# First down product kept ungated until the second's evacuation, with the modulation dots and two norms rescheduled

## The chip, the cores and the metric

The kernel runs as one program on one core of one Trainium2 chip. The metric is the device time of one execution in microseconds. The chip's engines are TensorE (PE in the profile, its weight loads PEld), VectorE (DVE), ScalarE (ACT), GpSimd (POOL) and SyncE (SP, which here only issues DMAs; "SPq" in the trace is its queue of issues).

## The reference, cut to what matters

One layer of a diffusion backbone works on 512 latent tokens `x` and 256 context tokens `ctx`, 1024 channels each. A modulation vector of nine sections of 1024 numbers is computed from a conditioning vector for x, and from another for ctx; the change touches how and when those sections are computed, and the first feed-forward sublayer with its residual and norm:

```python
mod_x = (jax.nn.silu(c) @ w_ada + b_ada).reshape(bsz, N_MOD, 1, d)
mod_c = (jax.nn.silu(c_ctx) @ w_ada + b_ada).reshape(N_MOD, 1, d)

def ffn_sublayer(h, m, i, w_up, w_down):
    shift, scale, gate = sub_mod(m, i)            # sections 3i, 3i+1, 3i+2
    y = swiglu(modulate(h, shift, scale), w_up, w_down)
    return post_ln(DEEPNORM_ALPHA * h + 0.5 * gate * y, ln_g[i], ln_b[i])

x = ffn_sublayer(x, mod_x, 0, ffn1_w_in, ffn1_w_out)
ctx = ffn_sublayer(ctx, mod_c, 0, ffn1_w_in, ffn1_w_out)
... = split_proj(modulate(x, shift_x, scale_x) @ w_in)   # z, q, k, v, gates, from sections 3 and 4
```

After that come neighbourhood attention and a gated delta rule, their merge, and a second feed-forward sublayer on x. The hidden width of the feed-forward is 2816, which is 22 tiles of 128. Everything is float32.

## The kernel before, in words

**Products.** A float32 product is made of three reduced products: an operand is split into a high part (a cast on ACT, L137: `wh`, `uh`, `hx`) and a low part (a subtraction on DVE, L139: `wl`, `ul`), and PE runs high by high, high by low and low by high. Each 128x1024 weight tile (512 KB) is loaded on SP (L174, helper `Stream`) into a raw tile `wr`, a ring of two slots in the pool `wp`, then cast and subtracted.

**Modulation.** A modulation section of 1024 is eight columns of 128, and each column is one step: a 512 KB piece of `w_adaT` is loaded (L296, on SP) and multiplied and summed along the row with the conditioning row on DVE (L280, 128x1024; one such "dot" for x and, for sections 2 to 4, a second for ctx). The generator `ada_gen` gives 48 such steps, for sections 2 to 7 in order; section 2 is the gate of this sublayer, 3 and 4 modulate the projections, and 5 to 7 are used later. Calls of `ada_step(n)` place them by hand: one or two per pass of the first loop, two in the context loop, two behind the last weights of the first down product, then by the tables ADA2 and ADA3. A finished gate section is turned into a row and stored by `rows_out` (`to_row`, L239).

**Stages around the change**, in order:

1. The x loop (L456): hidden tiles 3 to 7 of x, 512 tokens wide (tiles 0 to 2 are done earlier), with the context's own modulation `modulate_k` in between, and one ada step a pass (two in the last).
2. The context loop (L476): hidden tiles 0 to 7 for 256 tokens, with an ada step after tiles 0 and 2, then the row of gate section 2.
3. The first down product (L574): these 8 hidden tiles times their down weights, first x in 8 PSUM banks (4 token tiles by 2 halves), then ctx in 4. `down` (L196) keeps the banks open over all weights; its last KL weights, the tail, are taken token tile by token tile so that the banks end one after another. The evacuation loads the token rows (L584) and the gate row (`load_g`), and DVE forms alpha times token plus gate times product (L588, L589), which goes to the DRAM tile `accd`.
4. "Seven" (L606): the other 14 hidden tiles by a seven-product scheme; an ada step is placed by ADA2 after each. Hidden activations go to DRAM.
5. The second down product, x (L703): 14 hidden tiles come back (`hx`, loaded on SP by `h_next`), eight weights with all 8 banks, then a tail of six. Behind each of the eight weights `h_next` issues loads of later `hx` and `hc` tiles, of `accd` (tile `ax`, L697) and the ada steps of ADA3; their raw tiles are a ring of four of their own.
6. Evacuation `evac1`: per half a multiply by the gate (L635) and an add of `accd` with row sums (L636); then the norm `finish1` (two passes of 128x1024 on DVE, L649 and L651, with squares on ACT, L644, and the inverse root on POOL) and the modulated, transposed activations `u2` (transposes L148 on PE, L151 on ACT, then the split into `uxh` and `uxl`).
7. The second down product for ctx (L726) runs on PE meanwhile; FIN1 says behind which weights the four `finish1` and `u2` of x are issued. Its banks are evacuated in the same way into `x1c`.
8. The projections `z` (L1002), which read `uxh` and `uxl` of all four x tiles, then attention and the rest.

The program's order on each engine is fixed when it is built, by a scheduler that starts from the order of the code; DMA loads on SP are issued in SP's order, each when its slot is free.

## Time and profile before

| what | value |
|---|---|
| runs of the kernel | 1517.03, 1508.75, 1510.5 us; median 1510.5 |
| profiled execution | 1512.61 us, its span 1510.8 us |
| mean granted TensorE clock | 0.986 |
| DVE busy | 1149.5 us, 76% of the span |
| ACT busy | 662.8 us, 44% |
| DMA | 248.56 MB, mean 165 GB/s |

How to read the views in this document: a page's section 1 gives the busy time of each engine; a table by windows gives for each stretch of the span its length, the busy time (and count) of PE, PEld, DVE, ACT and POOL in us, the granted clock of PE, the busy share of the DMA engines and the GB/s that they moved. A chain of waits is followed back from the end of a stretch, a line for each piece: start, length, what ran or was waited for. A row of waits reads "engine, line <- what it waited for: us in total, times, longest". A group of instructions has line, engine, operation, tiles and shapes, count | busy us, mean ns of one | idle time before them and what ended it. A busy PE is not PE at its peak rate, so matmul counts per stretch say more than its busy share.

### The profile page before, as it was taken

The numbers are of one execution on the slowest core, as the hardware profiler recorded it, in microseconds if no ns is written. First come the engines' busy times: TensorE is split into PE (matmuls) and PEld (weight loads), VectorE is DVE, ScalarE is ACT, GpSimd is POOL, SyncE is SP. The second block draws the span as 40 slices with busy tenths as digits, with TensorE's granted clock in tenths as the row PEclk, the third lists the DMA queues.
The fourth block names the chain that finished last, engine by engine and source line by source line (L and its number), as shares of the span: only waits on it lengthen the run. The fifth ranks groups of instructions, "written<-read, shape, count | busy, mean of one in ns | idle before, by whom it ended". The sixth has DMA issues, their size and how long they took to land.

```text
span 1510.8 us, 23895 instructions
## 1 busy us (share of the span) xinstructions
PE 1441.6 (95%) x9117; PEld 1262.9 (84%) x9117; DVE 1149.5 (76%) x1975; ACT 662.8 (44%) x1090; POOL 211.2 (14%) x262
## 2 busy tenths in 40 slices
PE   6998999999999989999996998989999999999997
PEld 4778989999997778889875777867778999998886
DVE  8787869999988665778677795567669699886626
ACT  5433524434333386555534334267526454444310
POOL 1000000000000110313201001333221022220001
PEclk9999999999999999999998999999999999999999
DMA  9677664445469444222576514274344143233732
GB/s 375 207 262 232 209 236 171 156 164 167 165 231 397 157 153 134 92 78 91 175 214 183 168 64 124 72 261 146 100 168 144 60 136 107 98 112 121 269 98 83
DMA packets 114948, 248.56 MB, mean 165 GB/s; under 512 B 35145, under 2 KB 50577, under 8 KB 114833
## 3 DMA queue, kind: packets, MB, share of 16 engines
q1 hardware_dynamic: 110192, 229.40, 45.4%
q0 software_dynamic: 3056, 12.33, 2.2%
q10 hardware_dynamic: 1586, 5.32, 0.9%
q8 instruction: 71, 1.16, 0.3%
q14 instruction: 43, 0.35, 0.1%
HBM read 215.50 MB, written 31.50 MB: 163 GB/s over the span
## 4 chain that ended last, share of the span: by engine, by line
PE 69%; DVE 13%; DMA 10%; issue 4%; ACT 3%; POOL 1%; SPq 1%; DVEq 0%; ACTq 0%; POOLq 0%
PE ps L211 15%; PE ps L533 4%; PE ps L535 4%; PE ps L534 4%; PE pm L192 4%; PE pm L193 4%; PE pm L194 4%; PE ps L193 3%; PE ps L192 3%; PE ps L1679 3%; PE ps L194 3%; PE ps L1680 3%; PE ps L1681 3%; PE pc L1049 2%; DVE wl L139 2%
## 5 line engine op out<-in xcount | busy, mean ns | idle before, releaser
L139 DVE TENSOR_TENSOR wl<-wr,wh 128x1024 fp32r<-128x1024 f32 (+1 forms) x184 | 226.8, 1238 | 119.2 <-ACT wh L137 119.0
L137 ACT CAST wh<-wr 128x1024 fp32r<-128x1024 f32 (+1 forms) x184 | 185.9, 1015 | 265.7 <-PE pm L193 60.1
L192 PE MATMUL pm<-uxh,wh 128*128 128x512 f32 x320 | 132.4, 414 | 1.0 <-ACT spill L798 1.0
L194 PE MATMUL pm<-uxh,wl 128*128 128x512 f32 x320 | 127.2, 397 | 0.3 <-DVE wl L139 0.3
L193 PE MATMUL pm<-uxl,wh 128*128 128x512 f32 x320 | 127.1, 397 | 0.0
L211 PE MATMUL ps<-wh,hx 128*128 128x512 f32 x352 | 96.1, 391 | 0.9 <-ACT wh L137 0.9
L211 PEld LDWEIGHTS ps<-wh,hx 128*128 128x128 f32 x352 | 65.9, 188 | 15.3 <-ACT wh L137 1.3
L280 DVE SCALAR_TENSOR_TENSOR adap<-wr,crow 128x1024 f32<-128x1024 f32 x61 | 74.6, 1223 | 2.3 <-DMA wr<-in_w_adaT_dram 1.7
L192 PE MATMUL ps<-uh,wh 128*128 128x256 f32 (+1 forms) x208 | 68.6, 331 | 5.0 <-ACT wh L137 5.0
L194 PEld LDWEIGHTS pm<-uxh,wl 128*128 128x128 f32 x320 | 61.1, 191 | 14.3 <-DVE wl L139 1.3
L192 PEld LDWEIGHTS pm<-uxh,wh 128*128 128x128 f32 x320 | 61.5, 192 | 12.6 <-ACT spill L798 1.4
L193 PEld LDWEIGHTS pm<-uxl,wh 128*128 128x128 f32 x320 | 61.4, 192 | 10.6
L114 POOL TENSOR_TENSOR rs<-ve,mhalf 128x1 f32<-128x1 f32 (+2 forms) x46 | 48.2, 1050 | 140.7 <-DVE ve L110 138.3
L193 PE MATMUL ps<-ul,wh 128*128 128x256 f32 (+1 forms) x208 | 67.5, 326 | 0.0
L194 PE MATMUL ps<-uh,wl 128*128 128x256 f32 (+1 forms) x208 | 66.6, 325 | 0.0
L193 PE MATMUL ps<-uxl,wh 128*128 128x256 f32 (+1 forms) x192 | 61.6, 324 | 2.1 <-DVE uxl L139 2.1
L192 PE MATMUL ps<-uxh,wh 128*128 128x256 f32 (+1 forms) x192 | 60.7, 323 | 1.6 <-ACT uxh L137 1.4
L194 PE MATMUL ps<-uxh,wl 128*128 128x256 f32 (+1 forms) x192 | 61.1, 321 | 0.0
L137 ACT CAST wh<-ra 128x1024 fp32r<-128x1024 f32 x31 | 32.6, 1053 | 58.1 <-PE ps L534 20.2
L533 PE MATMUL ps<-ur,wh 128*128 128x384 f32 x168 | 56.5, 336 | 0.0
L534 PE MATMUL ps<-ur,wh 128*128 128x384 f32 x168 | 56.4, 336 | 0.0
L533 PE MATMUL ps<-uh,wh 128*128 128x384 f32 x168 | 56.4, 336 | 0.0
(498 smaller groups left out, 4264.4 us busy)
## 6 DMA issues: line engine op xcount, KB each, us to landing
wr<-in_w_adaT_dram SPq DMA_DIRECT2D x64, 512.0 KB, 4.8
wr<-in_up_dram SPq DMA_DIRECT2D x56, 512.0 KB, 3.7
wr<-in_win_dram SPq DMA_DIRECT2D x52, 512.0 KB, 3.4
wr<-in_dn_dram SPq DMA_DIRECT2D x51, 512.0 KB, 4.0
ra<-in_up_dram SPq DMA_DIRECT2D x24, 512.0 KB, 4.2
rb<-in_up_dram SPq DMA_DIRECT2D x18, 512.0 KB, 3.3
ra<-in_w_adaT_dram SPq DMA_DIRECT2D x16, 512.0 KB, 5.0
wr<-in_w_o_dram SPq DMA_DIRECT2D x8, 512.0 KB, 4.5
```

Source lines behind the costliest of these rows:

```text
L114: G.tensor_tensor(rs[:], ve[:], mhalf[:, 0:n], ALU.pow)
L137: S.copy(hi, src)
L139: marks["lo"] = V.tensor_tensor(lo, src, hi.bitcast(F32), ALU.subtract).ins
L192: T.matmul(ps, a, uh[:, k, :], start=(k == 0), stop=False)
L193: T.matmul(ps, a, ul[:, k, :], start=False, stop=False)
L194: marks["mm"] = T.matmul(ps, b, uh[:, k, :], start=False, stop=(k == nk - 1)).ins
L211: T.matmul(banks[t][d][:, c0:c1], a[:, sl], b[:, d * 512 + c0:d * 512 + c1], start=first and j == 0, stop=last and j == 2)
L280: V.scalar_tensor_tensor(pr[:], raw[:], 1.0, crow, op0=ALU.mult, op1=ALU.mult, accum_out=col[:, c:c + 1])
L533: T.matmul(ps[:], a, mh, start=k == 0, stop=False)
L534: T.matmul(ps[:], a, ml, start=False, stop=False)
L535: T.matmul(ps[:], b, mh, start=False, stop=k == 3)
L1679: T.matmul(ps[:], a, uh[:, k], start=k == 0, stop=False)
```

## The change

The first down product is no longer gated where it is made. ACT copies its 12 half tiles out of PSUM (`S.copy`, 128x512), and they go to `accd` as they are; the token and gate loads and the 24 DVE operations of that place go. In `evac1` each half now takes three DVE operations: product plus stored product, times gate, then alpha times token plus that, with row sums (new lines 628, 629, 630). The token rows are loaded there: `xr`, one tile, for x; a slot of the weights' `wr` ring for ctx.

The ada steps move: none in the x loop and the context loop (8 steps, 16 dots of section 2, were there), three in the first down product's tail, one in its context part, 21 instead of 25 in Seven, 16 instead of 13 in the second down product, and five new ones in the z loop. Gate section 2 is finished in Seven, and its rows are stored after Seven's fifth tile. The raw tiles of the ada steps in the second down product are now two tiles of their own and, every third time, a slot of the weights' ring; in the z loop they all use the weights' ring, and the dots read a copy of the conditioning row spread by a DMA (`arow`).

In the second down product, x tiles 0 and 1 are evacuated in the tail's own code, and their norms are issued ahead of the evacuations of tiles 2 and 3. FIN1 becomes (0, 2, 4, 6).

```diff
-    def ada_gen(tps, raw_of, crow):
+    rows_of = [lambda w: crow[:, w]]
+
+    def ada_gen(tps, raw_of):
...
-                        dot_cols(tps[0], raw, crow[:, w], col, sec * 8 + k, sec > 4)
+                        dot_cols(tps[0], raw, rows_of[0](w), col, sec * 8 + k, sec > 4)
...
-    ADA2 = (2, 1, 2, 1, 2, 1, 2, 2, 2, 2, 2, 2, 2, 2)
-    ADA3 = (2, 2, 2, 2, 2, 2, 2, 2)
+    ADA2 = (2, 1, 1, 2, 1, 1, 2, 1, 1, 2, 1, 2, 2, 2)
+    ADA3 = (2,) * 8
...
@@ -458,7 +460,6 @@
             modulate_k(pp, "c", k)
-        ada_step(1 + (f == N1 - 1))
@@ -476,8 +477,6 @@
         ffn_unit(tp, pp, ws.get(), ws.get(), uch, ucl, NCT, *hc[-1])
-        ada_step(f in (0, 2))
-    rows_out(tp, "fs", 2)
@@ -488,8 +487,14 @@
         else:
             ada_step()
-        if j == 0:
-            load_g(0)
+
+    def t_dots(j):
+        if j == 3:
+            ada_step()
+
+    def t_tail(t, j, banks):
+        if j == 1 and t < 3:
+            ada_step()
@@ -563,30 +568,16 @@
-    def load_g(w):
-        g[:] = [tl(tp, [P, 512], "fs", 2) for _ in range(2)]
...
-        if kind == "c":
-            load_g(1)
-        banks, tail = down(pp, ws, hs, n, 2 if kind == "x" else 0, tail if kind == "c" else (), between=t_sums if kind == "x" else None)
+        banks, tail = down(pp, ws, hs, n, 2 if kind == "x" else 0, tail if kind == "c" else (), between=t_sums if kind == "x" else t_dots, after=t_tail if kind == "x" else None)
...
-            nc.sync.dma_start(xr, tok_src(kind, t))
-            tmp = tl(tp, [P, D], "adap")
             for d in range(2):
-                sl = slice(d * 512, (d + 1) * 512)
-                V.tensor_tensor(tmp[:, sl], banks[t][d][:], g[d][:], ALU.mult)
-                V.scalar_tensor_tensor(xr[:, sl], xr[:, sl], ALPHA, tmp[:, sl], op0=ALU.mult, op1=ALU.add)
+                S.copy(xr[:, d * 512:(d + 1) * 512], banks[t][d][:])
             nc.gpsimd.dma_start(accd[t + 4 * (kind == "c")], xr)
@@ -614,6 +605,9 @@
         ada_step(ADA2[f], "h")
+        if f == 4:
+            with tc.issue_after(marks["mm"]):
+                rows_out(sgp, [8, P], "row")
@@ -627,13 +621,13 @@
-    def evac1(p, banks, acc, out, g):
+    def evac1(p, banks, acc, tok, g):
         out_sum, nm = tl(p, [P, 2], "os", 6), tl(p, [P, 1], "nm", 6)
         for d in range(2):
             sl = slice(d * 512, (d + 1) * 512)
-            h = tl(p, [P, 512], "h1", 2)
-            V.tensor_tensor(h[:], banks[d][:], g[:, sl], ALU.mult)
-            V.scalar_tensor_tensor(out[:, sl], h[:], 1.0, acc[:, sl], op0=ALU.mult, op1=ALU.add, accum_out=out_sum[:, d:d + 1])
+            V.tensor_tensor(acc[:, sl], banks[d][:], acc[:, sl], ALU.add)
+            V.tensor_tensor(acc[:, sl], acc[:, sl], g[:, sl], ALU.mult)
+            V.scalar_tensor_tensor(acc[:, sl], tok[:, sl], ALPHA, acc[:, sl], op0=ALU.mult, op1=ALU.add, accum_out=out_sum[:, d:d + 1])
@@ -695,44 +689,75 @@
+        if j == 7:
+            x_row()
         ada_step(ADA3[j])
 
+    xrs = []
+
+    def x_row():
+        xrs.append(tl(lp, [P, D], "xr"))
+        with tc.issue_after(marks["raw"]):
+            nc.sync.dma_start(xrs[-1][:], tok_src("x", len(xrs) - 1))
+
+    raws3 = [0]
+
+    def raw3():
+        raws3[0] += 1
+        k = raws3[0] % 3
+        return tl(ad, [P, D], f"w{k}") if k else tl(wp, [P, D], "wr", WB)
+
-    ada_tp[0], ada_raw[0] = ad, lambda: tl(ad, [P, D], "wr", 4)
+    ada_tp[0], ada_raw[0] = ad, raw3
     h_split(4)
-    bx, tail = down(pp, ws, hx, 4, KL1, between=h_next, n=N2)
+    nms = []
+
+    def x_after(t, j, banks):
+        if j == KL1 - 1 and t < 2:
+            nms.append(evac1(lp, banks, accx[t], xrs[t], gx))
+            x_row()
+
+    bx, tail = down(pp, ws, hx, 4, KL1, between=h_next, after=x_after, n=N2)
     h_split_c(N2)
-    for _ in ada:
-        pass
...
-    nms = [evac1(lp, bx[t], accx[t], accx[t], gx) for t in range(4)]
-    rows_out(lp, "h1", 2)
+    y1s = []
+    for t in range(2):
+        y1s.append(finish1(fc, "x", t, accx[t], nms[t]))
+        with tc.issue_after(marks["x2"]):
+            nms.append(evac1(lp, bx[t + 2], accx[t + 2], xrs[t + 2], gx))
+        if t == 0:
+            x_row()
+    rows_out(wp, [P, D], "wr", WB)
...
     def between(j):
         if j in FIN1:
             t = FIN1.index(j)
-            u2(fc, pp, "x", t, finish1(fc, "x", t, accx[t], nms[t]))
+            u2(fc, pp, "x", t, y1s[t])
+            if t < 2:
+                y1s.append(finish1(fc, "x", t + 2, accx[t + 2], nms[t + 2]))
 
     def after(t, j, banks):
         if j == NT - 1:
-            nms.append(evac1(lp, banks, x1c[t], x1c[t], gc))
+            raw = tl(wp, [P, D], "wr", WB)
+            nc.sync.dma_start(raw[:], tok_src("c", t))
+            nms.append(evac1(lp, banks, x1c[t], raw, gc))
 
-    FIN1 = (0, 2, 5, 8)
+    FIN1 = (0, 2, 4, 6)
...
@@ -837,6 +862,10 @@
+    arow = tl(ga_, [P, D], "arow")
+    nc.gpsimd.dma_start(arow[:], sild.broadcast_to([P, D]))
+    rows_of[0], ada_raw[0] = lambda w: arow[:], lambda: tl(wp, [P, D], "wr", WB)
...
         for _ in fill_spill(ga_, "z", m, zd):
             pass
+        ada_step((2, 2, 1, 0)[m])
```

**SP's order in the second down product, x.** Before, between the sixth weight of the product (`wr_4325`, just above this piece) and the eighth (`wr_4423`); `in_dn` are its weights, `in_w_adaT` the ada steps, `accd` the stored first product, `hd` hidden activations:

```order
L697 DMA ax_719_4075<-accd_1646 128x1024
L680 DMA hc_4461<-hd_2182 128x256
L174 DMA wr_4374<-in_dn_dram 128x1024
L697 DMA ax_720_4076<-accd_1646 128x1024
L680 DMA hx_4404<-hd_2182 128x512
L296 DMA wr_4270<-in_w_adaT_dram 128x1024
L296 DMA wr_4274<-in_w_adaT_dram 128x1024
L296 DMA wr_4319<-in_w_adaT_dram 128x1024
L680 DMA hx_4453<-hd_2182 128x512
L296 DMA wr_4322<-in_w_adaT_dram 128x1024
L680 DMA hx_4500<-hd_2182 128x512
L174 DMA wr_4423<-in_dn_dram 128x1024
```

The same piece now, between the sixth weight (`wr_4268`, just above) and the eighth (`wr_4366`):

```order
L691 DMA ax_701_4018<-accd_1586 128x1024
L298 DMA wr_4311<-in_w_adaT_dram 128x1024
L298 DMA w_754_4262<-in_w_adaT_dram 128x1024
L298 DMA w_755_4265<-in_w_adaT_dram 128x1024
L674 DMA hx_4446<-hd_2114 128x512
L174 DMA wr_4317<-in_dn_dram 128x1024
L691 DMA ax_702_4019<-accd_1586 128x1024
L298 DMA wr_4363<-in_w_adaT_dram 128x1024
L298 DMA w_763_4314<-in_w_adaT_dram 128x1024
L298 DMA w_770_4360<-in_w_adaT_dram 128x1024
L174 DMA wr_4366<-in_dn_dram 128x1024
```

Three ada loads and the last `hx` load moved ahead of the seventh weight, and one of every three ada loads takes a slot (`wr`) of the ring that the weights use. Counted over SP's order from the last of Seven's weight loads on, 13.89 MB are issued up to the seventh weight before and 16.25 MB now; up to the eighth weight 17.83 MB before and 18.87 MB now; up to the ninth 18.87 and 19.92.

**DVE's order at the end of the context part.** Before (`h` and `x1c` are the two evacuations, `uxl_4691<-u_929` the low part of the last x tile's activations, `wl` the low part of a z weight; those of the first two z weights stand two rows above this piece):

```order
L139 TENSOR_TENSOR uxl_4691<-u_905_4970,uxh_4690 128x4x128
L635 TENSOR_TENSOR h_935_5135<-ps_4747,g_4740 128x512
L139 TENSOR_TENSOR uxl_4691<-u_905_4970,uxh_4690 128x4x128
L636 SCALAR_TENSOR_TENSOR x1c_842_4742,os_5130<-h_934_5132,x1c_842_4742 128x512
L636 SCALAR_TENSOR_TENSOR x1c_842_4742,os_5130<-h_935_5135,x1c_842_4742 128x512
L637 TENSOR_SCALAR nm_5131<-os_5130 128x1
L635 TENSOR_TENSOR h_938_5165<-ps_4748,g_4740 128x512
L635 TENSOR_TENSOR h_939_5168<-ps_4749,g_4740 128x512
L636 SCALAR_TENSOR_TENSOR x1c_843_4743,os_5163<-h_938_5165,x1c_843_4743 128x512
L649 SCALAR_TENSOR_TENSOR x1c_842_4742<-x1c_842_4742,nm_5131,lng_4695 128x1024
L636 SCALAR_TENSOR_TENSOR x1c_843_4743,os_5163<-h_939_5168,x1c_843_4743 128x512
L139 TENSOR_TENSOR uxl_4691<-u_929_5071,uxh_4690 128x4x128
```

Now, from the evacuation of the last two banks (`ps_4756`, `ps_4757`) to the first z weight's low part (`wl_5139`):

```order
L628 TENSOR_TENSOR x1c_809_4667<-ps_4756,x1c_809_4667 128x512
L628 TENSOR_TENSOR x1c_809_4667<-ps_4757,x1c_809_4667 128x512
L629 TENSOR_TENSOR x1c_809_4667<-x1c_809_4667,g_4750 128x512 x2
L643 SCALAR_TENSOR_TENSOR x1c_808_4666<-x1c_808_4666,nm_5093,lng_4673 128x1024
L630 SCALAR_TENSOR_TENSOR x1c_809_4667,os_5127<-wr_5125,x1c_809_4667 128x512
L139 TENSOR_TENSOR uxl_4669<-u_904_4995,uxh_4668 128x4x128
L630 SCALAR_TENSOR_TENSOR x1c_809_4667,os_5127<-wr_5125,x1c_809_4667 128x512
L139 TENSOR_TENSOR uxl_4669<-u_904_4995,uxh_4668 128x4x128
L139 TENSOR_TENSOR wl_5139<-wr_5136,wh_5138 128x1024
```

The last x tile's `uxl` still stands behind the last evacuation, and the low part of the first z weight has moved from ahead of the evacuations to behind all of them.

**SP's order at the same place.** Before, the last three weights of the context part and the first z weights (`in_win`):

```order
L174 DMA wr_4993<-in_dn_dram 128x1024
L174 DMA wr_5011<-in_dn_dram 128x1024
L174 DMA wr_5029<-in_dn_dram 128x1024
L174 DMA wr_5172<-in_win_dram 128x1024
L174 DMA wr_5178<-in_win_dram 128x1024
L174 DMA wr_5257<-in_win_dram 128x1024
```

Now, from the last two weights of the context part on:

```order
L174 DMA wr_5018<-in_dn_dram 128x1024
L174 DMA wr_5036<-in_dn_dram 128x1024
L757 DMA wr_5090<-in_ctx_dram 128x1024
L757 DMA wr_5125<-in_ctx_dram 128x1024
L174 DMA wr_5136<-in_win_dram 128x1024
L833 DMA nw_5167<-in_norm_w_dram 128x1
L835 DMA cst_5169<-in_cst_dram 128x256
L174 DMA wr_5142<-in_win_dram 128x1024
```

The two context token tiles have come in ahead of the z weights in the ring of two slots, so that the first z weight takes the slot that the first context tile holds until its evacuation has read it, and the second z weight that of the second.

22 lines of the change are left out of this document (9 added, 13 removed).

## The prediction

> **What bounds the kernel now.** The page comes first, for what is busy over the span.
>
> ```profile
> span 1510.8 us, 23895 instructions
> PE 1441.6 (95%) x9117; PEld 1262.9 (84%) x9117; DVE 1149.5 (76%) x1975; ACT 662.8 (44%) x1090; POOL 211.2 (14%) x262
> ```
>
> PE is busy for 95%, so DVE work or loads taken away are worth only what PE waited for them. The table by windows says where PE waits, and its counts say where it runs slowly although it counts as busy.
>
> ```profile
> 110.00:115.00 5.00, 4.04 (x19) 3.03 (x18) 4.72 (x10) 3.10 (x6) 0.00 (x0) 1.00 0.77 215
> 120.00:125.00 5.00, 2.37 (x11) 1.88 (x11) 3.36 (x4) 2.27 (x3) 0.00 (x0) 0.78 0.11 32
> 125.00:130.00 5.00, 5.00 (x39) 5.00 (x39) 4.34 (x9) 1.51 (x3) 0.00 (x0) 0.87 0.89 284
> 130.00:135.00 5.00, 3.84 (x31) 3.43 (x29) 4.56 (x7) 1.91 (x3) 0.00 (x0) 1.00 0.82 254
> 135.00:140.00 5.00, 4.73 (x40) 4.74 (x41) 2.83 (x4) 2.80 (x5) 0.00 (x0) 1.00 0.85 298
> 140.00:145.00 5.00, 5.00 (x45) 5.00 (x44) 4.72 (x8) 1.36 (x2) 0.00 (x0) 1.00 0.72 237
> 140.00:240.00 100.00, 100.00 (x571) 88.74 (x570) 75.05 (x113) 38.59 (x56) 2.73 (x5) 1.00 0.64 221
> 240.00:440.00 200.00, 200.00 (x1151) 199.83 (x1150) 190.47 (x301) 78.43 (x104) 7.59 (x14) 1.00 0.48 164
> 440.00:490.00 50.00, 49.14 (x217) 40.32 (x216) 39.17 (x65) 17.33 (x29) 1.62 (x3) 1.00 1.01 382
> 490.00:520.00 30.00, 30.00 (x132) 24.18 (x131) 16.36 (x30) 5.45 (x6) 1.98 (x2) 1.00 0.43 151
> 520.00:550.00 30.00, 28.04 (x132) 22.19 (x131) 22.23 (x37) 27.04 (x47) 9.12 (x14) 1.00 0.56 200
> 570.00:580.00 10.00, 10.00 (x45) 8.23 (x45) 3.47 (x8) 7.47 (x11) 3.64 (x15) 1.00 0.27 98
> ```
>
> Three places matter. Between 120 and 140, in the context loop, PE waits and its clock falls to 0.78 and 0.87. In 440 to 490, the second down product for x, the DMA engines are full (1.01). From 520 the evacuations and norms overlap the context part. In Seven (240 to 440) PE never waits, with DVE busy for 190 of 200 us. The waits of PE from 60 to 640, grouped by what ended them, name the culprits:
>
> ```profile
> PE ps L192 <- ACT wh L137: 5.2, 6, 2.4
> PE ps L192 <- ACT uxh L137: 1.4, 1, 1.4
> PE ps L211 <- ACT wh L137: 1.3, 2, 0.9
> PE ps L148 <- ACT y L660: 1.1, 1, 1.1
> ```
>
> The 5.2 us are casts of up weights. Followed back, the chain of waits of 60 to 140 leads through loads, and ahead of these through dots:
>
> ```profile
> 116.14 1.24 DVE adap L280 x2
> 117.40 4.22 DMA wr<-in_up_dram
> 129.62 4.46 DMA wr<-in_up_dram
> ```
>
> The up weight's load at 117.40 starts as soon as an ada dot has let go: SP's queue is in order, and the ada loads, which wait for a slot, stand ahead of it.
>
> **The change part by part. Loops.** Eight steps leave the x and context loops, with 16 dots; the groups of DVE in 60 to 135 price a dot:
>
> ```profile
> L280 DVE SCALAR_TENSOR_TENSOR adap<-wr,crow 128x1024 f32<-128x1024 f32 x19 | 23.2, 1222 | 2.2 <-DMA wr<-in_w_adaT_dram 1.7 <-ACT crow L288 0.3
> ```
>
> That is 16 x 1.22 = 19.5 us of DVE and 4 MB of loads, none of it worth more than PE's loss. From 120 to 140 PE did 11 + 39 + 31 + 40 = 121 matmuls, where the stretch after it does 45 in 5 us, so 180: 59 are missing, at 5/45 = 0.111 us each, **-6.6 us**. With 0.96 us idle in 110 to 115 the most is -7.5; the least, if only half of the waits for weights go, I set at -3. The idle time alone is 2.63 + 1.16 + 0.27 = 4.1 us; the remaining 2.5 us is the lowered clock. The Trainium skill (TensorE: Matmul & The Clock Gate, "What's actually happening") puts the drop to half clock after an idle window of about 3.4 us. The trace differs: no wait here was over 2.4 us, and the clock was 0.78; by that rule waits this short cost no clock, and the loops would give 4.1 us rather than 6.6.
>
> **First evacuation.** The 24 DVE operations and the loads of token and gate rows become 12 copies on ACT, of which the copies in Seven are the nearest row:
>
> ```profile
> L547 ACT COPY c<-ps 128x384 f32<-128x384 f32 x7 | 3.4, 482 | 9.4 <-PE ps L535 9.4
> ```
>
> That is 12 x about 0.6 us on an engine that is busy for 44%, in a stretch where PE doesn't wait at all (100.00 of 140 to 240): 0. Seven keeps its dots (39 before, 39 now: 21 steps, of which more belong to sections with two dots), so its DVE stays just below full: 0; were it 2% fuller, PE would pay, at most 2 us. The two gate rows add small ACT work there: 0. The five z steps put 5 dots (6.1 us) and 2.5 MB into the z loop, where DVE is busy for 3.47 of 10 us and the DMA engines move 98 GB/s (570 to 580): 0, up to 2.
>
> **Second down product.** The chain of 440 to 480 ends in the eighth weight:
>
> ```profile
> 468.81 8.13 DMA wr<-in_dn_dram
> 477.03 1.05 ACT wh L137
> 478.12 1.90 PE ps L211 x7
> ```
>
> It lands at 476.95 and PE has waited 0.86 us for it (50.00 less 49.14). Up to it, 18.87 MB are now issued in place of 17.83; at the 382 GB/s of 440 to 490 the 1.04 MB are **+2.7 us**, and the wait that was there makes them all count. The seventh weight comes 2.36 MB, so 6.2 us, later; before, it was 3.94 MB (10.3 us) ahead of the eighth, so landed about 466.6, where PE wanted it a turn of 24 matmuls (at 49.14/217 us, 5.4 us) earlier than the eighth, that is at 470.7: it eats its own 4.1 us and then 2.1 of the same wait. The bound below is 0 (the stage drains by the tail), that above is the ring, under the rivals. In the Trainium skill (DMA: Bandwidth & Descriptors, "Where 436 GB/s comes from") the ports' ceiling is 435 GB/s; by it the 1.04 MB would be an estimated 2.4 us and the sum 0.3 less. No stretch quoted here passes 382 GB/s.
>
> **Evacuation of x.** The groups of DVE from 500 to 572 price it:
>
> ```profile
> L635 DVE TENSOR_TENSOR h<-ps,g 128x512 f32<-128x512 f32 x12 | 8.1, 686 | 4.0 <-PE ps L211 4.0
> L649 DVE SCALAR_TENSOR_TENSOR ax<-ax,nm,lng 128x1024 f32<-128x1024 f32 x4 | 5.1, 1282 | 0.0
> 510.44 1.29 DVE h L635 x2
> ```
>
> Two run in 1.29, so each takes about 0.60 of the queue, and 1024 wide 1.2. A tile now has six such halves, not four: 8 more for x, 4.8 us. DVE's idle 13.6 us of 490 to 520 hide those of tiles 0 and 1, if their tokens are there. Starting at 510.44, the new order reaches the first bank of tile 2 after 12 halves and two norm passes, at 510.44 + 7.2 + 2.4 + 0.2 = 520.2, and has read it at 520.9. The context part, which follows the x part at 517.0, wants that bank after 18 matmuls of 0.226 (49.14/217 in 440 to 490), at 521.1: just in time. But one of the halves waits for token tile 1, which has the same single buffer as tile 0, free at 515.2, and the ordinary load in this region takes:
>
> ```profile
> wr<-in_dn_dram SPq DMA_DIRECT2D x19, 512.0 KB, 4.2
> ```
>
> So it lands at 519.4, the bank is free at about 522.5, and PE waits 1.4 us. The low parts of the next context weights stand behind this on DVE, with tile 3's extra 1.2 us, so I take **+2.5 us**. Below, -1.1: FIN1 is earlier, and the wait for `y` goes. Above, +6, if tiles 2 and 3 each miss their tokens once more.
>
> **Start of z.** The chain from the end of the context part:
>
> ```profile
> 562.26 0.27 DVE h L635
> 564.15 1.20 DVE x1c L649
> 565.96 0.62 DVE uxl L139
> 566.62 0.79 PE ps L193
> ```
>
> PE begins 4.4 us after the last bank. Now DVE has two reads, two gate products, a norm pass, a half, `uxl`, a half, `uxl` and the first weight's low part: eight halves at 0.6 and two long ones at 1.2, 7.2 us: **+2.8 us**, since PE needs that low part in its first group. If PE finds enough to do without that low part, only the later `uxl` counts (4.8 us against 4.2), +0.6; if the z weight, whose slot a context tile holds until its last half, lands late, +5.
>
> The sum: -6.6 + 2.7 + 2.5 + 2.8 = **+1.4 us**. On the profiled execution that is 1512.6 + 1.4 = 1514.0; this execution is 2.1 above the median of 1510.5, and against the median it is **1512**. The runs before spread from 1508.75 to 1517.03, so a change under 0.5% (7.5 us), about what a measurement of this kernel can tell from no change, counts as none.
>
> **The rivals.**
>
> *Forecast*, the loops' gain given back at three later waits, 1506 to 1516: 0.52.
>
> *The gain stays.* The late waits don't come: the token loads are early, `uxl` is all that z waits for and the earlier FIN1 takes away the wait for `y` (1.1) and for `uxh` (1.4). With -7.5 that is -10.0, 1500.5. For it: DVE idles 13.6 us in 490 to 520, and the last x tile's transposes are issued two weights sooner. Against it: DVE's order puts its `uxl` behind the last evacuation anyhow. 0.13.
>
> *Slower: the ring of two slots.* In SP's order the sixth, seventh and eighth weight now take the same slot in turn, an ada tile the other. A slot is held for 8.1 us of load, 1.05 of cast and 1.2 of subtraction, 10.4 us, where PE takes 5.4 a weight: the seventh and eighth are each 5.0 late, +9.1 beyond the 0.86 that was there, and the clock falls as it did at 120 (0.22 + 0.13 of 5 us each, 1.7). With the other terms, -6.6 + 9.1 + 1.7 + 2.5 + 2.8 = +9.5, 1520. It decides if loads in this stage still take over 3.2 us (5.4 less 2.2) when a slot comes free; for it speaks the 1.01 share, against it that a shorter queue lands sooner, and that weights may be ahead by then. 0.25.
>
> *The loops give nothing.* Up weights are late for their own ring, not for the ada loads: -1 in place of -6.6, +7, 1517.5. Against it: ada dots and loads stand ahead of them in the chain. 0.10.
>
> **How the numbers follow.** Ends of the forecast's terms make -8 to +16 at the outside, never all together. From 1503 (part of the gain staying) to 1521 (the ring) some 0.8 are held: left out are most of 0.13 below and the worst of the ring above. Faster by over 7.5 us is the gain staying: 0.13. Slower by over 7.5 us is most of the ring and some of the last rival: 0.26. The rest is 0.61.
>
> **What would show it.** In the changed profile, PE without waits from 110 to 140 and the granted clock at 1.00 there, so that the second stages start 6 to 7 us sooner; in the second down product one or two waits for `wh` of 2 to 4 us in all (8 or more is the ring); a wait of about 1.4 us for a bank or a low part just behind the x part; and about 7 us from the last context bank to z's dense matmuls. The forecast is wrong if PE still waits in the context loop, or if z starts within 5 us.

## The result: slower, and the profile after

The changed kernel takes 1534.31 us (median of 4 runs, 1531.21 to 1538.07), the kernel before, run beside it, 1513.14 (1508.75 to 1517.03): a ratio of 1.0143, with a 95% interval of 1.0121 to 1.0165. That is outside the range of 1503 to 1521, on the slow side. The profiled execution took 1533.48 us, 20.9 more than that of before.

The first section of the page after:

```profile
span 1531.7 us, 23878 instructions
PE 1445.2 (94%) x9117; PEld 1262.3 (82%) x9117; DVE 1142.5 (75%) x1963; ACT 668.8 (44%) x1102; POOL 212.8 (14%) x263
```

DVE does 7.0 us less work, ACT 6.0 more. PE is busy for 3.6 us more with the same 9117 matmuls, and the other 17.3 of the 20.9 us are time in which it is idle. The table by windows after (columns as before):

```profile
120.00:125.00 5.00, 5.00 (x46) 5.00 (x45) 3.19 (x4) 2.38 (x4) 0.00 (x0) 1.00 0.37 120
125.00:130.00 5.00, 5.00 (x47) 5.00 (x46) 2.98 (x4) 2.25 (x5) 0.00 (x0) 1.00 0.59 197
440.00:490.00 50.00, 44.74 (x196) 36.05 (x194) 37.02 (x63) 14.61 (x24) 0.62 (x2) 1.00 0.97 362
520.00:550.00 30.00, 25.59 (x106) 18.99 (x106) 25.47 (x44) 26.06 (x43) 9.31 (x12) 0.94 0.72 240
590.00:600.00 10.00, 5.38 (x19) 4.24 (x18) 5.76 (x10) 4.03 (x10) 0.00 (x0) 0.70 0.61 192
```

In the context loop PE now does 46 and 47 matmuls per 5 us at full clock, where it did 11 and 39. But from 440 to 490 it does 196 in place of 217, and from 590 to 600, in the middle of z, only 19 at a clock of 0.70. Where each stage begins is read from the matmuls by line. The columns are: engine, operation, tiles and count, then shortest, median and longest duration in ns, start of the first and of the last. Before:

```profile
L533 PE MATMUL ps<-uh,wh x168: 332/336/339, 234.6 to 436.4; 128*128 128x384 f32 x168
L211 PE MATMUL ps<-wh,hx x224: 387/389/504, 439.0 to 516.8; 128*128 128x512 f32 x112
L211 PE MATMUL ps<-wh,hc x112: 387/389/504, 517.0 to 562.1; 128*128 128x512 f32 x112
L192 PE MATMUL ps<-uxh,wh x40: 387/389/628, 563.9 to 595.1; 128*128 128x512 f32 x40
L192 PE MATMUL pm<-uxh,wh x320: 387/389/795, 596.6 to 987.2; 128*128 128x512 f32 x160
```

The rows are Seven, the second down product for x, the same for ctx, the z loop (`ps`), and the projections behind it (`pm`). After:

```profile
L538 PE MATMUL ps<-uh,wh x168: 332/336/421, 227.5 to 429.5; 128*128 128x384 f32 x168
L211 PE MATMUL ps<-wh,hx x224: 387/389/499, 432.1 to 514.9; 128*128 128x512 f32 x112
L211 PE MATMUL ps<-wh,hc x112: 387/392/632, 515.1 to 565.0; 128*128 128x512 f32 x112
L192 PE MATMUL ps<-uxh,wh x40: 389/389/793, 568.6 to 609.9; 128*128 128x512 f32 x40
L192 PE MATMUL pm<-uxh,wh x313: 387/389/795, 611.4 to 999.4; 128*128 128x512 f32 x157
```

First starts subtracted give a ledger of the 20.9 us. Seven starts 7.1 earlier. The x part, from its start to that of the ctx part, takes 83.0 in place of 78.0 us: +5.0. From there to z it is 53.5 for 46.9: +6.6. The z loop takes 42.8 for 32.7: +10.1. What follows takes 920.3 for 914.2: +6.1. The largest loss, 10.1 of 27.8 us, lies in the z loop, where the prediction had put the new steps at 0.

The waits of PE from 440 to 640, after (us in total, times, longest):

```profile
PE ps L192 <- ACT wh L137: 7.8, 2, 4.6
PE ps L211 <- ACT wh L137: 6.3, 5, 2.7
PE ps L211 <- DVE nm L649: 2.2, 1, 2.2
```

Both large rows are casts of weights: the first in z (L192), the second in the down product (L211). In the down product, the chain of waits back from 490 shows why they are late (start, length, what):

```profile
454.52 4.30 DMA wr<-in_dn_dram
...
459.99 1.24 DVE wl L139
...
461.25 5.43 DMA wr<-in_dn_dram
...
467.83 1.24 DVE wl L139
...
469.08 5.71 DMA wr<-in_dn_dram
```

Each down weight's load begins within 0.02 us of the end of the subtraction of the one before it: three in a row pass through one slot, at 6.7 and 7.8 us each, where PE takes 5.4. The other slot holds an ada tile. The chain back from 612 in the z loop:

```profile
580.95 0.35 POOL convr L864 x9
581.30 8.25 DMA arow<-sild
589.57 1.25 DVE wr L280 x2
590.84 3.45 DMA wr<-in_win_dram
594.30 1.05 ACT wh L137
595.38 1.24 DVE wl L139
596.63 3.13 DMA wr<-in_w_adaT_dram
599.86 1.25 DVE wr L280 x2
601.12 4.46 DMA wr<-in_w_adaT_dram
...
606.93 4.74 DMA wr<-in_win_dram
```

A z weight waits for a dot, the dot for its ada tile, the ada tile for a z weight's subtraction: weights and ada tiles take turns in the two slots. The first dot waits for `arow` besides, whose load POOL issues only at 581.30, behind its own work; POOL's waits from 540 to 592 have one row:

```profile
POOL ve L112 <- ACT sq L638: 34.2, 7, 11.8
```

That is the norms' inverse roots, waiting for their squares; six of the seven waits, 32.1 us, stand in order ahead of that load.

The beginning of z has a loss of its own. Rows of the timeline (start, length, engine, line, operation, count; in brackets the idle time before and what ended it), and SP's longest wait from 555 to 612:

```profile
563.68 0.33 SPq L174 DMA_DIRECT2D wr<-in_win_dram  x1
565.18 1.29 DVE L628 TENSOR_TENSOR x1c<-ps,x1c 128x512 f32<-128x512 f32 x2 [1.28 <-PE ps L211]
568.57 0.50 PE L192 MATMUL ps<-uxh,wh 128*128 128x512 f32 x1 [3.20 <-ACT wh L137]
572.49 0.79 PE L194 MATMUL ps<-uxh,wl 128*128 128x512 f32 x1 [1.59 <-DVE wl L139]
```

```profile
SPq L174 <- DVE nm L631: 13.0, 1, 13.0
```

SP waits 13.0 us with the first z weight, until the first context tile has been read out of its slot, and z begins only when that weight has landed and is cast. From the read of the last two context banks (565.18) to the first matmul with the weight's low part (572.49), behind which z is dense, there are 7.3 us; before, there were 4.4 (562.26 to 566.62). So 1.2 of the z loop's 10.1 us belong to its beginning.

### The profile page after: what moved, and what is told of

Its sections match the earlier page's. It is cut to its first block, busy times and chain, and to the rows that moved or that the text cites. A ratio compares the mean times of both kernels' runs of the same rounds, so it can differ in the third digit from the quotient of the medians.

```text
span 1531.7 us, 23878 instructions
## 1 busy us (share of the span) xinstructions
PE 1445.2 (94%) x9117; PEld 1262.3 (82%) x9117; DVE 1142.5 (75%) x1963; ACT 668.8 (44%) x1102; POOL 212.8 (14%) x263
## 3 DMA queue, kind: packets, MB, share of 16 engines
q1 hardware_dynamic: 109616, 228.35, 45.3%
## 4 chain that ended last, share of the span: by engine, by line
PE 66%; DVE 12%; DMA 11%; issue 6%; ACT 3%; POOL 2%; SPq 1%; DVEq 0%; POOLq 0%; ACTq 0%
PE ps L211 15%; PE ps L540 4%; PE pm L192 4%; PE ps L538 4%; PE ps L539 4%; PE pm L194 4%; PE pm L193 4%; PE pc L1079 3%; PE ps L194 3%; PE ps L193 3%; PE ps L192 2%; PE ps L1709 2%; PE ps L1711 2%; PE ps L1710 2%; DVE wl L139 2%
## 5 line engine op out<-in xcount | busy, mean ns | idle before, releaser
L192 PE MATMUL pm<-uxh,wh 128*128 128x512 f32 x320 | 132.1, 413 | 1.1 <-ACT spill L823 1.0
L211 PE MATMUL ps<-wh,hx 128*128 128x512 f32 x352 | 96.4, 391 | 5.3 <-ACT wh L137 5.3
L280 DVE SCALAR_TENSOR_TENSOR adap<-wr,crow 128x1024 f32<-128x1024 f32 x64 | 78.1, 1220 | 7.6 <-DMA wr<-in_w_adaT_dram 7.1
L211 PEld LDWEIGHTS ps<-wh,hx 128*128 128x128 f32 x352 | 65.8, 188 | 20.4 <-ACT wh L137 6.5
L192 PEld LDWEIGHTS pm<-uxh,wh 128*128 128x128 f32 x320 | 61.0, 190 | 12.5 <-ACT spill L823 1.4
L193 PEld LDWEIGHTS pm<-uxl,wh 128*128 128x128 f32 x320 | 61.1, 191 | 10.4
L192 PE MATMUL ps<-uxh,wh 128*128 128x256 f32 (+1 forms) x192 | 61.5, 326 | 7.8 <-ACT wh L137 7.8
L192 PE MATMUL ps<-uh,wh 128*128 128x256 f32 (+1 forms) x208 | 67.0, 322 | 0.0
L539 PE MATMUL ps<-ur,wh 128*128 128x384 f32 x168 | 56.4, 336 | 0.0
L539 PE MATMUL ps<-ul,wh 128*128 128x384 f32 x168 | 56.4, 336 | 0.0
```

The costliest lines, as they stand in the source:

```text
L192: T.matmul(ps, a, uh[:, k, :], start=(k == 0), stop=False)
L193: T.matmul(ps, a, ul[:, k, :], start=False, stop=False)
L211: T.matmul(banks[t][d][:, c0:c1], a[:, sl], b[:, d * 512 + c0:d * 512 + c1], start=first and j == 0, stop=last and j == 2)
L280: V.scalar_tensor_tensor(pr[:], raw[:], 1.0, crow, op0=ALU.mult, op1=ALU.mult, accum_out=col[:, c:c + 1])
L539: T.matmul(ps[:], a, ml, start=False, stop=False)
```

## The experiments

The theory formed on this ledger: the loops give what they were to give, and the ring of two slots, lent to ada tiles in the down product and in z, to the context tokens and to the gate's row, gives it back and more. The rivals: bytes rather than slots; the late `arow`; and the evacuation itself (its third DVE operation, its token loads, the norms' new order). Letters in the expectations name theories: A is the ring lent out, D the single token buffer, F the third operation with the token loads, H the steps' places alone; where another letter stands, the expectation says what it is. Edits are against the changed kernel unless another is named. All the runs in one table, with the stages worked out from each trace as above (us; "rest" is from the end of z to the end of the span):

| kernel | Seven starts | x part | ctx part to z | z loop | rest | median | ratio to before (95%) |
|---|---|---|---|---|---|---|---|
| before | 234.6 | 78.0 | 46.9 | 32.7 | 914.2 | 1513.14 | 1 |
| after | 227.5 | 83.0 | 53.5 | 42.8 | 920.3 | 1534.31 | 1.0143 (1.0121 to 1.0165) |
| e1_noz | 229.3 | 82.3 | 53.9 | 35.2 | 914.6 | 1521.67 | 1.0066 (1.0045 to 1.0087) |
| e2_arow_sp | 229.6 | 81.2 | 53.9 | 40.9 | 923.5 | 1535.06 | 1.0140 (1.0115 to 1.0165) |
| e4_ctxown | 228.5 | 82.9 | 54.8 | 36.5 | 920.1 | 1526.65 | 1.0086 (1.0059 to 1.0114) |
| e5_raw4 | 228.8 | 76.9 | 56.6 | 35.3 | 910.2 | 1517.49 | 1.0034 (1.0013 to 1.0054) |
| e6_rowown | 227.8 | 82.0 | 56.2 | 38.9 | 910.5 | 1521.46 | 1.0051 (1.0033 to 1.0069) |
| e7_free | 227.4 | 76.9 | 61.6 | 31.7 | 913.6 | 1518.89 | 1.0039 (1.0024 to 1.0055) |
| e8_freeord | 228.9 | 76.8 | 59.7 | 31.4 | 914.9 | 1517.99 | 1.0039 (1.0026 to 1.0052) |
| e9_loops | 234.7 | 78.6 | 50.5 | 36.7 | 913.0 | 1520.84 | 1.0057 (1.0041 to 1.0074) |
| e10_two | 229.1 | 76.8 | 58.7 | 30.6 | 911.3 | 1511.50 | 0.9998 (0.9982 to 1.0013) |
| e11_twoord | 229.5 | 76.9 | 64.2 | 31.8 | 906.7 | 1518.63 | 1.0042 (1.0026 to 1.0058) |
| e12_notok | 228.0 | 86.3 | 51.6 | 43.9 | 915.4 | 1530.04 | 1.0120 (1.0095 to 1.0144) |
| e13_ord | 226.2 | 82.5 | 56.4 | 38.2 | 913.8 | 1526.30 | 1.0102 (1.0070 to 1.0133) |
| e14_ev2 | 229.7 | 76.8 | 52.0 | 33.4 | 910.6 | 1510.16 | 0.9992 (0.9979 to 1.0005) |
| e15_ev2ord | 229.5 | 76.9 | 52.4 | 34.1 | 912.5 | 1510.47 | 0.9992 (0.9980 to 1.0005) |
| e16_steps | 230.0 | 77.4 | 46.3 | 32.7 | 904.8 | 1502.65 | 0.9941 (0.9925 to 0.9956) |
| e17_ev2all | 226.9 | 76.9 | 52.3 | 34.3 | 908.9 | 1509.64 | 0.9978 (0.9963 to 0.9994) |
| e18_notail | 226.6 | 81.7 | 47.0 | 32.8 | 914.0 | 1509.96 | 1.0007 (0.9989 to 1.0024) |

The column "rest" moves by up to 19 us between kernels that have no edit there, so small differences of a median are not evidence for a stage; the stages' own columns are. These have a spread too: in the 16 kernels whose two loops are those of the changed kernel, Seven starts between 226.2 and 229.7, 228.3 in the mean.

**The z steps left out** (their section, 7, is zero there).

```diff
+    G.memset(colx[:, 56:64], 0.0)
...
-        ada_step((2, 2, 1, 0)[m])
```

> The changed kernel without its five ada steps in the z loop (their section's modulation is left at zero, so five loads and five dots are left out). Theory A, the z steps lock the weights' ring of two while their dots wait for the spread conditioning row: PE's waits between 590 and 610 go, matmuls from the z loop on come 9 to 12 us sooner than in the changed kernel, about 1523. Rival B, z starts late because the context tiles hold the ring and VectorE's order is long: at most 2 us sooner, about 1532.

The z loop falls from 42.8 to 35.2, the whole by 12.6. The matmuls of z there (this kernel's lines stand one further down):

```profile
L193 PE MATMUL ps<-uxh,wh x40: 389/389/796, 570.1 to 603.7; 128*128 128x512 f32 x40
```

So the five steps cost 7.6 us in the loop itself, not 0 to 2.

**The conditioning row loaded by SP, earlier.**

```diff
+    nc.sync.dma_start(arow[:], sild.broadcast_to([P, D]))
...
-    nc.gpsimd.dma_start(arow[:], sild.broadcast_to([P, D]))
```

> The conditioning row's spread is loaded on SP, right behind the first two ada loads of the z loop, not on GpSimd behind the norms and the memsets; nothing else moves. Theory A, if the late row is what counts: the dots start at about 584 instead of 589.6 and the rest follows 4 to 6 us sooner, about 1529. If the shared ring itself counts (any ada tile in it costs a weight), 1 us or less, about 1533. Rival B: no change.

The chain of waits there:

```profile
580.46 4.57 DMA arow<-sild
...
586.39 6.77 DMA wr<-in_win_dram
...
595.52 3.25 DMA wr<-in_w_adaT_dram
...
600.13 4.33 DMA wr<-in_w_adaT_dram
```

The row is there 4.5 us sooner, the dots start at 585.1 rather than 589.6, and the loop is only 1.9 us shorter: the taking of turns in the ring remains. The lateness of the row explains some 2 of the 10 us.

**Context tokens in a buffer of their own**, that of x's tokens.

```diff
-            raw = tl(wp, [P, D], "wr", WB)
+            raw = tl(lp, [P, D], "xr")
```

> The two context token tiles use the single buffer of the x token tiles instead of two slots of the weights' ring. Theory A: the first z weight is there before the context part ends, z's dense matmuls start 3 to 6 us sooner, but the stall at 590 to 610 stays since the row's load stays behind the norms; part of the gain is lost there, about 1530 to 1533. Rival B: the whole z loss goes, 12 us or more sooner, about 1521.

The z loop is 6.3 us shorter and the whole 7.7. z does not start earlier, although its first weight is now cast at 555.7 rather than 567.4; what it waits for now is the high part of the last x tile:

```profile
570.81 1.65 PE L192 MATMUL ps<-uxh,wh 128*128 128x512 f32 x3 [4.44 <-ACT uxh L137]
```

So the tokens' slots delayed the first z weight as well as later ones, but at z's start two waits end close together, and freeing the slots alone gains nothing there.

**A ring of four again for the ada tiles of the second down product.**

```diff
-    ada_tp[0], ada_raw[0] = ad, raw3
+    ada_tp[0], ada_raw[0] = ad, lambda: tl(ad, [P, D], "w", 4)
```

> The ada steps of the second down product use a ring of four tiles of their own again; their number and places stay. If the 5 us lost between 450 and 480 come from the slots that ada tiles take in the weights' ring: 4 to 5 us sooner from 480 on, about 1529. If they come from the bytes issued ahead of the weights (1.04 MB more): 1 us or less.

The x part is 6.1 us shorter with the same loads and the same bytes in the same stage:

```profile
L211 PE MATMUL ps<-wh,hx x224: 387/389/398, 433.4 to 510.0; 128*128 128x512 f32 x112
```

From 440 to 490 the DMA engines move 394 GB/s where they moved 362, and PE does 222 matmuls without a wait. So what PE waited for there was the slot, not the bytes. The total falls by 16.8, far more than the 4 to 5 expected, and the z loop by 7.5, which the edit doesn't touch in the code; the scheduler's order behind it is another, and how much of that is the ring isn't told apart.

**The gate's row through `crow`** instead of the ring.

```diff
-    rows_out(wp, [P, D], "wr", WB)
+    while rows_due:
+        to_row(crow[0:8, 0, 0:P], pp, *rows_due.pop(0))
```

> The changed kernel, with the row of gate section 5 built in the conditioning row's tile (no longer read then) and not in a slot of the weights' ring. Theory A, the ring of two is what loses time behind the x part of the second down product too: the wait of a down weight for the row's store goes, 2 to 4 us sooner from 520 on, and z is not touched, so 1530 to 1532. Rival C, VectorE's longer evacuation and the single token buffer lose that time: under 1 us.

13 us faster, but at no place where it was expected: ctx part to z is even longer (56.2), z is 3.9 shorter, and 9.8 come from the rest. What this row cost by itself isn't settled.

**The ring lent to nobody**: the three edits above together, and the z steps put into the x part's tail.

```diff
+        if t == 0 and j < 5:
+            ada_step()
...
-    arow = tl(ga_, [P, D], "arow")
-    nc.gpsimd.dma_start(arow[:], sild.broadcast_to([P, D]))
...
-        ada_step((2, 2, 1, 0)[m])
```

> All borrowers leave the weights' ring at once: a ring of four for the ada tiles of the second down product, the context tokens in the x tokens' buffer, the row of section 5 in the conditioning row's tile, and the five z steps issued in the x part's tail with the same ring of four. Theory A, the ring explains nearly all: the loops' 7 us stay, the second down product's 5 us and the z part's 16 us go, the evacuation keeps 2 to 3 us; 1505 to 1512, level with the kernel before or up to 0.5% faster. Rivals B and C, VectorE's order behind the context part and the evacuation: 1517 or more.

The x part (76.9) and z (31.7) are now as short as before or shorter, and Seven starts 7.2 earlier; still the kernel is not faster. All of it goes into one stage, ctx part to z, 61.6 for 46.9. PE's waits from 440 to 640 there:

```profile
PE ps L148 <- ACT y L654: 7.8, 1, 7.8
PE ps L192 <- ACT uxh L137: 6.1, 1, 6.1
```

The casts of weights are gone from the head of the list, and in their place stand the norms' results: `y` for the transposes, `uxh` for z. z starts at 570.5, later than after's 568.6, although the ctx part began 6 us sooner.

**The same with the norms behind all evacuations** and FIN1 = (0, 2, 5, 8), as before the change.

```diff
-        y1s.append(finish1(fc, "x", t, accx[t], nms[t]))
-        with tc.issue_after(marks["x2"]):
-            nms.append(evac1(lp, bx[t + 2], accx[t + 2], xrs[t + 2], gx))
+        nms.append(evac1(lp, bx[t + 2], accx[t + 2], xrs[t + 2], gx))
...
-    FIN1 = (0, 2, 4, 6)
+    FIN1 = (0, 2, 5, 8)
```

> As the run with all borrowers out of the ring, with the norms of the x tiles issued again behind all four evacuations and placed as before (FIN1 0, 2, 5, 8). If putting two norms ahead of the last evacuations costs the context part its banks (rival C): 2 to 4 us sooner than that run. By theory A: within 1.5 us of it.

No difference in the median beyond the intervals. With the single token buffer, the norms' place isn't what makes `uxh` late.

**The freed ring, with the eight steps back in the loops.** Against e7_free:

```diff
+        ada_step(1 + (f == N1 - 1))
...
+        ada_step(f in (0, 2))
```

> As the run with all borrowers out of the ring, with the eight ada steps put back into the x and the context loop (so the last ones, in the x part's tail and more, fall away). If the loops' gain comes from taking these steps out: 6 to 7 us later than that run from 140 on, of which the lighter second down product may give 1 or 2 back.

Seven starts at 234.7, 7.3 later, which is the loops' gain shown by itself (4.9 to 8.4 over the 16 kernels named under the table):

```profile
L540 PE MATMUL ps<-uh,wh x168: 332/336/421, 234.7 to 436.7; 128*128 128x384 f32 x168
```

But the total is only 2 us worse, and z starts at 568.5, 2 us earlier than in e7_free. This isn't a test of the loops alone: there are 48 steps in all, so the last eight calls, the five in the x part's tail among them, do nothing here, and the last ada load of the second down product is issued at 474.9 rather than 497.5. With the three operations and the token loads all in place, ctx part to z falls from 61.6 to 50.5. What e7_free gains by Seven it has lost again by the time that z starts, and the longer evacuation alone doesn't explain that.

**Two token buffers**, the second in a free half of `crow`, each load issued a tile earlier; in e10_two with e7_free's order, in e11_twoord with e8_freeord's.

```diff
-        xrs.append(tl(lp, [P, D], "xr"))
+        xrs.append(crow[:, 1] if len(xrs) % 2 else tl(lp, [P, D], "xr")[:])
...
+            if t == 0:
+                x_row()
...
-            raw = tl(wp, [P, D], "wr", WB)
+            raw = crow[:, 1] if t else tl(lp, [P, D], "xr")[:]
```

> As the run with all borrowers out of the ring (1518.9), with two buffers in turn for the token tiles of x and ctx (the second is half of the conditioning row's tile). In that run z still lost 13 us, because the last x tiles' norms came late: 7.8 us of waiting for y, 6.1 for the high part. Theory D, the single token buffer delays the evacuations and with them the norms: the second to fourth evacuation come 3 to 6 us sooner, both waits shrink to a half or less, 1508 to 1512. Rival E, the order of the norms on ScalarE alone is what is late: within 2 us of 1518.9.

> As the run with two token buffers, with the norms behind all four evacuations and FIN1 0, 2, 5, 8 as before. If norms ahead of the last evacuations help once tokens are early: 1 to 4 us slower than that run; if they harm: as much faster. Theory D: both under 1514.

With the norms ahead the total is 1511.5, but the stage only falls from 61.6 to 58.7, and waits for `y` (9.9) and `uxh` (3.8) remain: the single buffer was at most 3 us of it. With the norms behind it is 7 us slower, so here their place does matter.

**The changed kernel without x's token loads** (x's residual is left out: the third operation reads the sum in place of the tokens).

```diff
-        xrs.append(tl(lp, [P, D], "xr"))
-        with tc.issue_after(marks["raw"]):
-            nc.sync.dma_start(xrs[-1][:], tok_src("x", len(xrs) - 1))
+        xrs.append(None)
```

> The changed kernel without the x token loads in the second evacuation: its third operation reads the sum itself in place of the tokens, so the residual is left out, with the same work on VectorE. Theory D: the evacuation's loss of 5 us (480 to 550) goes for the most part and z is reached 3 to 6 us sooner; the ring's other losses stay: 1524 to 1530. Rival C, VectorE's third operation: under 1.5 us sooner.

Ctx part to z gains 1.9 and the x part loses 3.3: the tokens alone are not it.

**The changed kernel with the norms behind** (the edit of e8_freeord on it).

> The changed kernel with the norms behind all four evacuations and FIN1 0, 2, 5, 8; all else as changed. If the new order of norms causes part of the loss: 3 us or more faster than 1534; if it helps a little: up to 3 us slower. Theories A and D expect it within 3 us of 1534.

The median is 8 us lower, where theories A and D expected it within 3; the intervals of the two ratios overlap (up to 1.0133 here, from 1.0121 there). In the one profiled execution z is 4.6 shorter and ctx part to z 2.9 longer. With the ring lent out, each new order moves several waits at once.

**The freed ring with the old evacuation**: two operations, no token loads (residual left out, and the stored first product not gated).

```diff
-            V.tensor_tensor(acc[:, sl], banks[d][:], acc[:, sl], ALU.add)
-            V.tensor_tensor(acc[:, sl], acc[:, sl], g[:, sl], ALU.mult)
-            V.scalar_tensor_tensor(acc[:, sl], tok[:, sl], ALPHA, acc[:, sl], op0=ALU.mult, op1=ALU.add, accum_out=out_sum[:, d:d + 1])
+            h = tl(p, [P, 512], "h1", 2)
+            V.tensor_tensor(h[:], banks[d][:], g[:, sl], ALU.mult)
+            V.scalar_tensor_tensor(acc[:, sl], h[:], 1.0, acc[:, sl], op0=ALU.mult, op1=ALU.add, accum_out=out_sum[:, d:d + 1])
```

> As the run with all borrowers out of the ring, with the evacuation of the kernel before: two operations a half and no token loads (so the residual and the gate on the first part are left out; the norms run as they do). Theory F, the third operation and the token loads make the norms late: z starts 8 us or more sooner than in that run, 1508 to 1511. Rival G, the order of norms and evacuations: at most 4 us sooner, 1515 or more.

> As the run before it, with the norms behind the last two evacuations and FIN1 0, 2, 5, 8. Theory F: within 3 us of it. Rival G: 5 us or more faster than it.

8.7 us faster than e7_free, and it shows where it was expected: ctx part to z falls from 61.6 to 52.0, and PE's waits from 440 to 640 to

```profile
PE ps L148 <- ACT y L654: 2.2, 2, 1.6
PE ps L192 <- ACT uxh L137: 1.6, 1, 1.6
```

So in this arrangement the third operation and its tokens, together, are 8.7 to 9.6 us of lateness. That is not their price everywhere: e9_loops, which has both and no steps in the tail, is only 3.6 above the kernel before in this stage (50.5 and 46.9). With the norms behind (e15_ev2ord) it is the same within 1 us. Both still start z 5 us later than the kernel before, counted from the ctx part's start.

**The same with all four evacuations behind the x part**, as before the change (e17_ev2all); and this with four steps moved from the x part's tail back into Seven, with the old ADA2 (e18_notail). Both leave out what e14_ev2 does.

```diff
-    ADA2 = (2, 1, 1, 2, 1, 1, 2, 1, 1, 2, 1, 2, 2, 2)
+    ADA2 = (2, 1, 2, 1, 2, 1, 2, 2, 2, 2, 2, 2, 2, 2)
...
-        if t == 0 and j < 5:
+        if t == 0 and j < 1:
             ada_step()
```

> As the run before it, with the evacuations of x tiles 0 and 1 issued behind the whole x part too, as in the kernel before: nothing of the second down product's end is changed any more but the stored product's content and the ring of four. Both theories: the 7 us of the loops show at the end, 1503 to 1507. If z still starts late here, neither holds, and the end of the x part with its moved ada steps is what delays the norms.

> As the run with the old evacuation in the old order, with four of the five ada steps of the x part's tail done in Seven as in the kernel before (ADA2 as it was). If the steps in the tail make the norms late: z starts 4 us or more sooner, and the whole is 1502 to 1505. If it is the scheduler's order at the end of the context part: z within 2 us of that run, 1508 to 1511, and ScalarE's last activations again wait for a low part that stands on VectorE behind the context evacuation.

e17_ev2all gains hardly more than e14_ev2, and z waits 7.4 us for `uxh`. Its timeline of ACT shows the last tile's activations waiting:

```profile
557.27 2.91 ACT L151 ACTIVATE u<-ps,colx 128x128 f32<-128x128 f32 x8 [2.30 <-DVE uxl L139]
```

They wait for a `uxl` of the tile before. e18_notail brings ctx part to z back to 47.0, but its x part takes 81.7, and z starts at 560.0 as in e17_ev2all (560.7). Do the five dots in the tail delay the norms by 5 us? The first read of an x bank in e17_ev2all speaks against it:

```profile
505.52 1.29 DVE L629 TENSOR_TENSOR h<-ps,g 128x512 f32<-128x512 f32 x2 [3.49 <-PE ps L211]
```

DVE is done with its dots by 502.0 and waits 3.5 us for PE to end that bank. In e18_notail the same read is at 504.29. From it to z's start there are 55.2 us in e17_ev2all and 55.7 in e18_notail, with and without four of the dots; 53.5 in the kernel before (from 510.44) and 53.3 in e16_steps below. So z's start follows this read, and the norms behind it take some 2 us more than before. The rest of the 5 us is that in e17_ev2all the read comes only 2.9 us ahead of the ctx part's start, where it came 6.6 ahead before. Why PE ends its first banks so late in the x part there stays open.

**The kernel before, with ada steps moved by two places only.** Against the kernel before: none in place of two in the last pass of the x loop, and in the context loop one behind each of the tiles 3 to 6 in place of tiles 0 and 2. There are eight in the two loops, as before.

```diff
-        ada_step(1 + (f == N1 - 1))
+        ada_step(f < N1 - 1)
...
-        ada_step(f in (0, 2))
+        ada_step(2 < f < 7)
```

> The kernel before, with only the eight ada steps of the x and context loops placed differently: one behind each of the x loop's first four passes, none behind its last, and one behind each of the context loop's tiles 3 to 6. Theory H, the context loop's first weights wait behind the ada loads issued at its start: 4 to 6 us faster than before, 1505 to 1508. If the loops' gain needs the steps out of both loops: within 2 us of 1511.

It is the fastest of all: 1502.65 us, a ratio of 0.9941 (0.9925 to 0.9956). PE's waits from 60 to 170, where the kernel before had 5.0 us for up weights alone, and the windows there:

```profile
PE ps L242 <- DVE colc L303: 1.4, 1, 1.4
PE ps L192 <- ACT wh L137: 0.6, 1, 0.6
```

```profile
120.00:130.00 10.00, 10.00 (x88) 10.00 (x87) 5.46 (x8) 4.96 (x7) 0.00 (x0) 1.00 0.63 214
130.00:140.00 10.00, 10.00 (x88) 10.00 (x86) 6.00 (x7) 4.42 (x8) 0.00 (x0) 1.00 0.59 204
```

The matmuls of its z loop:

```profile
L192 PE MATMUL ps<-uxh,wh x40: 389/389/628, 558.1 to 589.3; 128*128 128x512 f32 x40
```

Seven starts 4.6 us earlier and z 5.8 earlier: nothing of the gain is lost on the way, since the ring, the evacuation and the norms are as they were. At 1502.65 it is also below the 1505 to 1508 expected. The ratio stands for about 9 us in all, of which z's start explains 5.8; the other 3 lie behind z, where this kernel has no edit, and aren't explained. (In the one profiled execution, the fastest of five, the rest is even 9.4 shorter.)

## Why the prediction was wrong, point by point

- **Loops, -6.6: right.** Measured -7.1, and 7.3 in e9_loops against e7_free; over the 16 kernels with these loops 4.9 to 8.4, 6.3 in the mean. The working holds too: each of them is above the 4.1 us of idle time, so the slow matmuls came back as well. (Of the 5.2 us of casts, 5.0 are up weights; 0.2 lie in z.)
- **First evacuation and Seven, 0: right.** Seven takes 204.6 us from its start to the x part's, before 204.4.
- **Second down product, +2.7: half the size, and the wrong mechanism.** Measured +5.0. The step priced the bytes ahead of the eighth weight; the forecast kept the ring for a rival. With the same bytes and a ring of four for the ada tiles (e5_raw4) the x part is 6.1 us shorter and PE does 222 matmuls where it did 196. It is the rival's mechanism, at 6.7 to 7.8 us a weight rather than the 10.4 it was priced at, since loads landed in 4.3 to 5.7 us, not 8.1.
- **Evacuation of x, +2.5: half the size.** From the ctx part's start to the read of its last banks it is 50.1 us for 45.3, +4.8. The forecast wait for a low part is there (2.2 us, put down to `nm` L649, for 1.4); in all PE waits 4.2 us here where it waited 2.0. Most of the rest is the granted clock, 0.94 from 520 to 550, for which this term had nothing. With the ring freed this stage got longer, not shorter (e7_free), so the term's size is no general price of the third operation. The wait for `y`, which was to go at the lower bound, fell from 1.1 to 0.5.
- **Start of z, +2.8: right, with its mechanism.** 7.3 us for 4.4 from the last banks' read to dense matmuls, +2.9, and the last wait is the forecast one, for the first weight's low part behind the evacuation. The late first weight, which the prediction kept for its upper bound, came too (3.2 us of waiting at 568.57), and was hidden behind this.
- **The step that failed: "The five z steps put 5 dots (6.1 us) and 2.5 MB into the z loop ... 0, up to 2".** Measured +10.1, of which 1.2 is the later start above. It priced DVE's and the DMA engines' free time there, both of which exist, and not the slots: in the z loop the ada tiles share the two slots of `wr` with the z weights, and stay in them until a dot has read them. Without the five steps the loop takes 35.2 (-7.6); with the row of conditioning earlier, 40.9 (-1.9); with the context tokens out of the ring, 36.5 (-6.3). These don't add up, as each alone frees a slot.
- **Not foreseen: +6.1 behind z.** Counted by matmuls, some 4 of it appear right behind the loop: 28.6 us behind it (at 640) 158 are done, where before 152 were done after 23.4 us and 164 after 25.4. It was not tested by itself; e1_noz has 914.6, so 0.4, but e2_arow_sp 923.5 with the same z steps, so no more is to be read from it.
- **The rivals.** "The ring of two slots" named the cause, in the down product alone, and its 1520 is too small because z is missing in it (its down term, 10.8, was twice the 5.0 measured): the prediction knew that z's ada tiles use the ring and didn't carry the rival there. "The gain stays" failed by the late norms, and not only by the ring: e7_free frees it and is no faster than the kernel before. "The loops give nothing" is refuted.

So the change's gain early is real and its losses are three: the ring (about 5 in the x part, 7.6 to 8.9 in z), the longer evacuation with its tokens (3.6 to 9.6, by which kernels are compared), and about 5 us ahead of z that remain with the old evacuation: some 2 in the norms, the rest in where PE ends the first x banks, for a reason that stays open. The losses are not sums of independent terms, as e6_rowown and e5_raw4 show, where stages change that the edit doesn't touch.

## What to carry to other kernels

When a transfer is put into a ring of buffers that another stream uses, price the slot and not the bytes: how long it is held, from the load's start to its last reader, against how soon the stream needs it back (here 6.7 to 7.8 us a weight against 5.4). Carry a mechanism found at one place to every place where the change uses the same resource; the z steps were priced by free engine time alone, although they were known to use the ring, and that step failed. If an early wait is caused by where a few instructions stand, move these alone first: two edited lines gave 0.9941, where the whole change gave 1.0143.

## What the runs showed of the hardware that was not expected

- The granted clock falls after quite short waits. Before, no wait in the context loop was over 2.4 us, and 120 to 125 had 0.78. After, with a wait of 4.6 us in z, 590 to 600 had 0.70; without waits (the context loop after, and e16_steps) it was 1.00. The Trainium skill (TensorE: Matmul & The Clock Gate, "What's actually happening") gives an idle window of about 3.4 us for the drop: z agrees with it, the context loop of before does not.
- A load that POOL issues comes as late as POOL's own work ahead of it: `arow` was issued at 581.30 and landed at 589.55, behind 32.1 us of waits for squares. The same load on SP took 4.57 us rather than 8.25.
- The stages behind the z loop took between 904.8 and 923.5 us in 19 kernels. For the same 6155 or 6156 matmuls there PE is busy for 863.0 us in e16_steps and for 871.1 in e2_arow_sp, so 8 of their 18.7 us are slower matmuls and the rest waits. A ledger by stages is needed to tell a change of 5 us here; a total alone isn't enough.
